# Modulation columns in whole tiles of 1024 instead of two halves of 512, with bias and scale for eight columns at once

## The chip, the cores and the metric

The kernel runs on one core of a Trainium2 chip. The core has five engines that run side by side, each with a queue of its own that it works off in order: TensorE (PE in the profile; its weight loads are PEld), VectorE (DVE), ScalarE (ACT), GpSimd (POOL) and SyncE (SP), which here issues nearly all DMA transfers. They wait for each other by semaphores. The metric is the time of one execution in device microseconds (us).

## The reference

A trunk of two layers over a sequence of 512 tokens with 1024 features, in float32. A vector `c` sets, per layer, six modulation vectors of 1024: shift, scale and gate for the attention, and the same for the MLP.

```python
sc = jax.nn.silu(c)
for layer in range(DEPTH):
    mod = sc @ w_mod[layer] + b_mod[layer]
    shift1, scale1, gate1, shift2, scale2, gate2 = [m[:, None, :] for m in jnp.split(mod, 6, axis=-1)]
    h = rmsnorm(x, g_attn[layer]) * (1.0 + scale1) + shift1
    o = mixer_layer(h, w_in[layer], w_out[layer], diff_lambda[layer], ...)
    x = x + gate1 * o
    h = rmsnorm(x, g_mlp[layer]) * (1.0 + scale2) + shift2
    up = h @ w_up[layer]
    u, g = up[..., :D_FF], up[..., D_FF:]
    g = causal_depthwise_conv(g, conv_w[layer], conv_b[layer])
    x = x + gate2 * ((jax.nn.silu(g) * u) @ w_down[layer])
return rmsnorm(x, g_final)
```

`mixer_layer` is one input projection, three kinds of attention heads (A differential, B dilated windows, C forgetting) and one output projection. The factor of the differential heads comes from `diff_lambda`.

## The kernel before

**Layout.** Features lie on the 128 partitions and tokens in the free dimension, so a vector of 1024 features is eight columns of a 128-row tile. Matrix products run at float32 accuracy as three products of split operands: each weight tile comes by DMA as `raww`, ACT rounds it to `whi` (line 174), DVE takes the rest as `wlo` (line 186), and `mm3` (lines 264 to 267) issues high x high, high x low and low x high. Activations are split in the same way (`hh` and `hl`, lines 313 and 314, for the normalised input).

**Stages.** Start-up computes shift1 and scale1 of layer 0 from the tiles `mu`. Then follow, for each layer, `layer_attn` and `layer_mlp`. In `layer_attn` a loop over `b` takes 64 blocks of attention (8 pairs of heads, 2 heads, 4 blocks of 128 queries) in a software pipeline: scores `s` (`emit_S`), their masked maximum on DVE (`emit_max`, line 653, `nm`), the exponential on ACT (`emit_exp`, line 666, `e`), for kind A a combination of two maps on DVE (`emit_norm`, lines 679 to 681, `rd`), the transposes on TensorE (`emit_T`, line 694, `pt`), their split into `pth` on ACT and `ptl` on DVE (lines 713 and 718), and the product with the values (`emit_PV`, lines 740 and 741, `po`). Between them `fill` puts the projections of the next heads. `head_post` finishes a head (`op`, line 753, and on).

**The modulation columns.** One column `ci` of the 48 of a layer is a dot product of 128 rows of `w_mod` (1024 long, `wmod[l, ci]`) with `silu(c)`, which `scb` holds on all partitions. `mod_col` (line 211) does it in two halves of 512. Each half is loaded into a tile `rawm` of the pool `mrp` (three buffers, line 240). In the attention of layer 0 (columns 16 to 39) POOL multiplies it with `scb` (line 221), ACT sums it by its accumulator (line 224), and DVE adds the sum to the bias or to the first half (line 226). Elsewhere, in the MLP of layer 0 (columns 40 to 47 and all 48 of layer 1), one DVE instruction does product and sum (line 228). The columns of the two scale vectors are turned into `scl = (1 + scale) * g` one by one (line 234). From then on `h_part` reads `modc` and `scl`, and `gated_add` (line 326) reads the gates.

**What sets the order.** `mod_gen` turns the columns into a generator of small steps. In the attention the loop over `b` takes `mr` = 3.2 steps per block from block `ms` = 4 on (lines 848 to 851); in the MLP each `tick()` takes one. A scheduler then puts each engine's instructions into its queue in an order of its own, by priority and by what it reckons to be ready; on the chip every queue is worked off strictly in that order. A load into a buffer that is still read waits in SP's queue, and so does all that stands behind it there.

`lp`, the tile for `diff_lambda`, is loaded at start-up (line 1061) and read by `prep` (line 366) in block 10 of layer 0.

## Time and profile before

| | us |
|---|---|
| median of 3 runs | 1345.78 (1345.72 to 1348.15) |
| span of the profiled execution, first to last instruction | 1343.3 |
| start-up, until the first score maximum | 70.2 |
| attention of layer 0, until its last `x` | 70.2 to 318.7 |
| MLP of layer 0 | to about 680 |
| attention of layer 1, until its last `x` | to 963.4 |
| MLP of layer 1 and final norm | to 1343.3 |

The profile gives no time of the profiled execution apart from its span; the median of the runs is 2.5 us above it. How to read the rows that follow: in the tables of groups a row has the line, the engine, the operation, output<-inputs, the shapes, the number of instructions, then their busy time and mean duration in ns, then the idle time of the engine ahead of them and what ended it. In the timelines a row has the start and the duration in us, and in brackets the idle time ahead. Durations of neighbours overlap a little; from start to start is how long an instruction holds its queue. Busy TensorE means that a matmul was in its pipeline.

The stretch of DVE's queue at which the attention of layer 0 ends and its MLP begins is one of the places that matter below; the first half columns of the MLP stand in it.

### The profile page before, as it was taken

How to read it: one execution, taken by the hardware profiler on the slowest of the kernel's cores; microseconds unless marked ns; L12 is line 12 of the kernel's file. 1: busy time of each engine (PE TensorE's matmuls, PEld its weight loads, DVE VectorE, ACT ScalarE, POOL GpSimd, SP SyncE). 2: the span in 40 equal slices, each digit the busy share in tenths (PEclk: the TensorE clock that was granted, in tenths of full speed). 3: DMA queues.
4: the chain of work that ended last, by engine and by line, in shares of the span. 5: the costliest groups of instructions: out<-in, count | busy, mean ns of one | idle time of the engine just before them, and what ended most of it. 6: DMA issues, size and time to landing. Idle time of an engine off the chain costs nothing.

```text
span 1343.3 us, 18226 instructions
## 1 busy us (share of the span) xinstructions
PE 1289.3 (96%) x6568; PEld 1058.5 (79%) x6568; DVE 869.7 (65%) x1733; ACT 663.8 (49%) x1242; POOL 92.3 (7%) x64
## 2 busy tenths in 40 slices
PE   3899898999999999999999999999999999999997
PEld 1678787688888888888898888878978888888886
DVE  7888989868888886422357687875754444443332
ACT  5567888954433333322345676775543333333231
POOL 5222423400000000000000000000000000000000
PEclk8899999999999999999999999999999999999999
DMA  9344453432777774233422234212123232222331
GB/s 374 142 142 150 162 155 130 133 116 85 252 250 257 249 252 139 91 98 99 130 83 94 85 105 123 79 59 83 54 94 94 95 96 97 100 91 91 101 100 63
DMA packets 68127, 174.44 MB, mean 130 GB/s; under 512 B 9410, under 2 KB 11730, under 8 KB 68036
## 3 DMA queue, kind: packets, MB, share of 16 engines
q1 hardware_dynamic: 66884, 172.16, 39.3%
q8 instruction: 52, 0.85, 0.3%
q10 hardware_dynamic: 1088, 1.05, 0.2%
q14 instruction: 39, 0.32, 0.1%
q0 software_dynamic: 64, 0.06, 0.0%
HBM read 159.41 MB, written 2.10 MB: 120 GB/s over the span
## 4 chain that ended last, share of the span: by engine, by line
PE 68%; DVE 5%; ACT 3%; issue 2%; DMA 1%; SPq 0%; DVEq 0%; ACTq 0%
PE pu L265 6%; PE pg L266 6%; PE pg L267 6%; PE pu L267 6%; PE pu L266 6%; PE pg L265 6%; PE dps L265 6%; PE dps L267 6%; PE dps L266 6%; PE qkps L265 2%; PE ops L266 2%; PE ops L265 2%; PE ops L267 2%; PE qkps L266 2%; PE qkps L267 2%
## 5 line engine op out<-in xcount | busy, mean ns | idle before, releaser
L186 DVE TENSOR_TENSOR wlo<-raww,whi 128x1024 fp32r<-128x1024 f32 (+3 forms) x188 | 229.5, 1221 | 238.2 <-ACT whi L174 234.2
L174 ACT ACTIVATE whi<-raww 128x1024 fp32r<-128x1024 f32 (+3 forms) x188 | 194.5, 1035 | 344.3 <-PE dps L266 138.0
L266 PE MATMUL pg<-hl,whi 128*128 128x512 f32 (+1 forms) x368 | 143.0, 389 | 0.4 <-DVE hl L314 0.2
L265 PE MATMUL pg<-hh,whi 128*128 128x512 f32 (+1 forms) x368 | 141.5, 385 | 1.6 <-ACT whi L174 1.6
L265 PE MATMUL pu<-hh,whi 128*128 128x512 f32 (+1 forms) x368 | 142.3, 387 | 0.0
L267 PE MATMUL pg<-hh,wlo 128*128 128x512 f32 (+1 forms) x368 | 140.9, 383 | 1.1 <-DVE wlo L186 1.1
L266 PE MATMUL pu<-hl,whi 128*128 128x512 f32 (+1 forms) x368 | 140.7, 382 | 0.0
L267 PE MATMUL pu<-hh,wlo 128*128 128x512 f32 (+1 forms) x368 | 140.6, 382 | 0.0
L265 PE MATMUL dps<-mh,whi 128*128 128x512 f32 x308 | 121.5, 395 | 0.0
L267 PE MATMUL dps<-mh,wlo 128*128 128x512 f32 x308 | 121.5, 394 | 0.0
L266 PE MATMUL dps<-ml,whi 128*128 128x512 f32 x308 | 121.2, 393 | 0.0
L666 ACT ACTIVATE e<-e,nm 128x256 f32<-128x256 f32 (+3 forms) x160 | 88.9, 556 | 32.4 <-DVE nm L653 30.5
L265 PE MATMUL qkps<-hh,whi 128*128 128x512 f32 x224 | 98.3, 439 | 0.6 <-ACT qf L467 0.2
L653 DVE CUSTOM_DVE_ANT_0 e<-s,cst 128x256 f32<-128x256 f32 (+3 forms) x160 | 76.8, 483 | 21.3 <-PE s L632 9.2
L906 ACT ACTIVATE y<-y 128x512 f32<-128x512 f32 x44 | 27.8, 632 | 126.3 <-DVE y L903 116.7
L266 PE MATMUL qkps<-hl,whi 128*128 128x512 f32 x224 | 89.5, 400 | 0.0
L267 PE MATMUL qkps<-hh,wlo 128*128 128x512 f32 x224 | 89.0, 397 | 0.0
L267 PEld LDWEIGHTS pu<-hh,wlo 128*128 128x128 f32 x368 | 69.1, 188 | 16.5 <-DVE wlo L186 1.1
L266 PEld LDWEIGHTS pg<-hl,whi 128*128 128x128 f32 x368 | 69.0, 188 | 16.6 <-DVE hl L314 2.0
L267 PEld LDWEIGHTS pg<-hh,wlo 128*128 128x128 f32 x368 | 69.0, 188 | 16.5 <-DVE wlo L186 1.9
L265 PEld LDWEIGHTS pg<-hh,whi 128*128 128x128 f32 x368 | 69.2, 188 | 16.0 <-ACT whi L174 2.0
L221 POOL TENSOR_TENSOR rawm<-rawm,scb 128x512 f32<-128x512 f32 x48 | 69.5, 1458 | 163.4 <-DMA rawm<-in_wmod_dram 119.5
(182 smaller groups left out, 2814.7 us busy)
## 6 DMA issues: line engine op xcount, KB each, us to landing
raww<-in_wup_dram SPq DMA_DIRECT2D x88, 512.0 KB
rawm<-in_wmod_dram SPq DMA_DIRECT2D x160, 256.0 KB
raww<-in_wqk_dram SPq DMA_DIRECT2D x32, 512.0 KB
raww<-in_wdown_dram SPq DMA_DIRECT2D x32, 512.0 KB
mu<-in_wmod_dram SPq DMA_DIRECT2D x16, 512.0 KB
raww<-in_wout_dram SPq DMA_DIRECT2D x16, 448.0 KB
raww<-in_wv_dram SPq DMA_DIRECT2D x12, 512.0 KB
raww<-in_wdown_dram SPq DMA_DIRECT2D x16, 384.0 KB
```

The costliest lines, as they stand in the source:

```text
L174: A.activation(out=h[:, 0:m], in_=self.raw[i][:, c:c + m], func=AF.Copy)
L186: V.tensor_tensor(out=lo[:, 0:m], in0=raw[:, c:c + m], in1=h[:, 0:m].bitcast(F32), op=ALU.subtract)
L221: G.tensor_tensor(out=raw, in0=raw, in1=scb[:, 512 * half:512 * half + 512], op=ALU.mult)
L265: T.matmul(ps[:, c], w[0], rhs[0][:, c], start=first, stop=False, skip_group_check=True)
L266: T.matmul(ps[:, c], w[0], rhs[1][:, c], start=False, stop=False, skip_group_check=True)
L267: T.matmul(ps[:, c], w[1], rhs[0][:, c], start=False, stop=last, skip_group_check=True)
L653: anchor[0] = V.tensor_tensor_reduce(out=e[:, 0:n], in0=s[:, 0:n], in1=cst[:, mask + SEQ - n:mask + SEQ], scale=-scale, scalar=3e38, op0=A ...
L666: anchor[1] = A.activation(out=e[:, 0:n], in_=e[:, 0:n], func=AF.Exp, bias=nm, scale=-1.0, accum_out=den).ins
L906: last_silu[0] = A.activation(out=y, in_=y, func=AF.Silu).ins
```

## The change

`mod_col` and `mod_stream` become one generator. A column is one tile of 128x1024, one load, and one instruction on POOL and on ACT, or one on DVE. The bias of columns 16 to 39, and the scales, are done for eight columns in one DVE instruction when the last of the eight is ready (`m` = 7). `mrp` has two buffers of 1024 instead of three of 512. `lp` is no longer a tile of its own: in block 6 it takes a buffer of `mrp`, is loaded there, and is read by `prep` in block 10. The columns are taken at `mr` = 1.3 steps per block, with three steps per column in place of eight.

```diff
@@ -63,7 +63,7 @@
     hs = ctx.enter_context(tc.tile_pool(name="hs", bufs=28))
     rawp = ctx.enter_context(tc.tile_pool(name="rawp", bufs=3))
     wp = ctx.enter_context(tc.tile_pool(name="wp", bufs=2))
-    mrp = ctx.enter_context(tc.tile_pool(name="mrp", bufs=3))
+    mrp = ctx.enter_context(tc.tile_pool(name="mrp", bufs=2))
     tp = ctx.enter_context(tc.tile_pool(name="tp", bufs=4))
     sp = ctx.enter_context(tc.tile_pool(name="sp", bufs=1))
     sm = ctx.enter_context(tc.tile_pool(name="sm", bufs=8))
@@ -107,7 +107,7 @@
     cb = const.tile([128, DEPTH, FC], F32, name="cb")
     sg = const.tile([128, DEPTH], F32, name="sg")
     fb = const.tile([128, DEPTH, 6], F32, name="fb")
-    lp = const.tile([128, DEPTH, 4, 32], F32, name="lp")
+    lpt = []
     modc = const.tile([128, DEPTH, 48], F32, name="modc")
     scl = const.tile([128, DEPTH, 2, KC], F32, name="scl")
     nlam = const.tile([128, DEPTH], F32, name="nlam")
@@ -208,38 +208,32 @@
 
     W = Weights()
 
-    def mod_col(l, ci, raws, pool=False):
+    def mod_stream(l, ci):
         part, m = divmod(ci, 8)
-        prev = bm[:, l, ci:ci + 1]
-        for half in range(2):
-            raw = raws(half)
-            yield
-            dst = modc[:, l, ci:ci + 1]
-            if half == 0:
-                dst = sm.tile([128, 1], F32, tag="mp", name="mp")
-            if pool:
-                G.tensor_tensor(out=raw, in0=raw, in1=scb[:, 512 * half:512 * half + 512], op=ALU.mult)
-                yield
-                d2 = sm.tile([128, 1], F32, tag="mp", name="mq")
-                A.activation(out=raw, in_=raw, func=AF.Copy, accum_out=d2)
-                yield
-                V.tensor_tensor(out=dst, in0=d2, in1=prev, op=ALU.add)
-            else:
-                V.tensor_tensor_reduce(out=raw, in0=raw, in1=scb[:, 512 * half:512 * half + 512], scale=1.0, scalar=prev,
-                                       op0=ALU.mult, op1=ALU.add, accum_out=dst)
-            prev = dst
-            yield
+        pool = l == 0 and 16 <= ci < 40
+        raw = mrp.tile([128, 1024], F32, tag="raw", name="rawm")
+        nc.sync.dma_start(out=raw, in_=wmod[l, ci])
+        yield
+        dst = modc[:, l, ci:ci + 1]
+        if pool:
+            G.tensor_tensor(out=raw, in0=raw, in1=scb, op=ALU.mult)
+            yield
+            A.activation(out=raw, in_=raw, func=AF.Copy, accum_out=dst)
+        else:
+            V.tensor_tensor_reduce(out=raw, in0=raw, in1=scb, scale=1.0, scalar=bm[:, l, ci:ci + 1],
+                                   op0=ALU.mult, op1=ALU.add, accum_out=dst)
+            yield
+            yield
+        yield
+        if m < 7:
+            return
+        c = slice(8 * part, 8 * part + 8)
+        if pool:
+            V.tensor_tensor(out=modc[:, l, c], in0=modc[:, l, c], in1=bm[:, l, c], op=ALU.add)
         if part in (1, 4):
             g = gA if part == 1 else gM
-            V.scalar_tensor_tensor(out=scl[:, l, part // 4, m:m + 1], in0=modc[:, l, ci:ci + 1], scalar=1.0,
-                                   in1=g[:, l, m:m + 1], op0=ALU.add, op1=ALU.mult)
-
-    def mod_stream(l, ci):
-        def raws(half):
-            raw = mrp.tile([128, 512], F32, tag="raw", name="rawm")
-            nc.sync.dma_start(out=raw, in_=wmod[l, ci, :, 512 * half:512 * half + 512])
-            return raw
-        return mod_col(l, ci, raws, l == 0 and 16 <= ci < 40)
+            V.scalar_tensor_tensor(out=scl[:, l, part // 4, :], in0=modc[:, l, c], scalar=1.0,
+                                   in1=g[:, l, :], op0=ALU.add, op1=ALU.mult)
 
     def mod_gen(units, off):
         for l, u in units:
@@ -364,6 +358,7 @@
         return st
 
     def prep():
+        lp = lpt[0]
         for l in range(DEPTH):
             lam_init = 0.8 - 0.6 * math.exp(-0.3 * l)
             V.tensor_scalar(out=sg[:, l:l + 1], in0=sg[:, l:l + 1], scalar1=1.0 - lam_init, scalar2=None, op0=ALU.mult)
@@ -820,6 +815,10 @@
             while idx and fills[idx - 1][0]:
                 fill(idx - 1, 1.0)
             p = b - lag
+            if l == 0 and b == 6:
+                lpt.append(mrp.tile([128, 1024], F32, tag="raw", name="lp")[:, 0:256].rearrange(
+                    "p (l j d) -> p l j d", l=DEPTH, j=4))
+                nc.sync.dma_start(out=lpt[0], in_=lamp)
             if l == 0 and b == 10:
                 with tc.issue_after(anchor[0]), tc.issue_after(anchor[1]):
                     prep()
@@ -845,7 +844,7 @@
             fill(idx, f3)
             if p >= 0:
                 emit_PV(p)
-            ms, mr = 4, 3.2
+            ms, mr = 4, 1.3
             if b >= ms:
                 for _ in range(int((b - ms + 1) * mr) - int((b - ms) * mr)):
                     next(modg, None)
@@ -1058,7 +1057,7 @@
             st = attn_init(0, unit, ps0)
             W.pt = None
             with tc.issue_after(last_load[0]):
-                for t, a in ((fb, fbias), (cst, consts), (lp, lamp), (sg, sublng), (gM, gmlp), (gF, gfin), (cw, convw),
+                for t, a in ((fb, fbias), (cst, consts), (sg, sublng), (gM, gmlp), (gF, gfin), (cw, convw),
                              (cb, convb)):
                     nc.sync.dma_start(out=t, in_=a)
         for l in range(DEPTH):
```

Where the order changes, at the places that the prediction uses. The rows are one engine's instructions in the order of its queue; a row has the line, the operation, output<-inputs and the shape (ISA is the DVE instruction of lines 228 and 653 and the read of its accumulator). Lines of the changed kernel stand some five lower between 240 and 815, so that its L308 is L314 before, and its L661 is L666.

DVE at the end of the norm that opens the MLP of layer 0, before:

```order
L314 SCALAR_TENSOR_TENSOR hl<-ht,modc,hh 128x256
L228 ISA rawm,modc<-rawm,scb,mp 128x512
L228 ISA modc 128x1
L314 SCALAR_TENSOR_TENSOR hl<-ht,modc,hh 128x256
L228 ISA rawm,mp<-rawm,scb,bm 128x512
L228 ISA mp 128x1
L228 ISA rawm,modc<-rawm,scb,mp 128x512
L228 ISA modc 128x1
L186 TENSOR_TENSOR wlo<-raww,whi 128x1024
```

The same place in the changed kernel:

```order
L308 SCALAR_TENSOR_TENSOR hl<-ht,modc,hh 128x256
L223 ISA rawm,modc<-rawm,scb,bm 128x1024
L223 ISA modc 128x1
L308 SCALAR_TENSOR_TENSOR hl<-ht,modc,hh 128x256
L223 ISA rawm,modc<-rawm,scb,bm 128x1024
L223 ISA modc 128x1
L186 TENSOR_TENSOR wlo<-raww,whi 128x1024
```

One whole column stands ahead of the last `hl` where a half stood, and one between it and `wlo` where two halves stood. A whole column also stands some sixteen rows earlier, behind the fourth `hl`, where the first half stood.

ACT in the first blocks of the attention of layer 0, from the first column on, before:

```order
L224 ACTIVATE rawm,mq<-rawm 128x512
L666 ACTIVATE e,dens<-e,nm 128x128
L174 ACTIVATE whi<-raww 128x1024
L666 ACTIVATE e,dens<-e,nm 128x256
L467 ACTIVATE qf<-qkps 128x512
L666 ACTIVATE e,dens<-e,nm 128x384
L666 ACTIVATE e,dens<-e,nm 128x512
L713 ACTIVATE pth<-pt 128x384
```

And in the changed kernel:

```order
L221 ACTIVATE rawm,modc<-rawm 128x1024
L661 ACTIVATE e,dens<-e,nm 128x128
L174 ACTIVATE whi<-raww 128x1024
L661 ACTIVATE e,dens<-e,nm 128x256
L462 ACTIVATE qf<-qkps 128x512
L661 ACTIVATE e,dens<-e,nm 128x384
L221 ACTIVATE rawm,modc<-rawm 128x1024
L708 ACTIVATE pth<-pt 128x384
```

The second column now stands ahead of `pth` and of the exponential of 128x512, which follows two rows later.

## The prediction

> **What bounds the kernel now.** I read the busy table first, then the busy time by stage, then TensorE's waits, and last the groups of instructions of the columns.

> ```profile
> PE 1289.3 (96%) x6568; PEld 1058.5 (79%) x6568; DVE 869.7 (65%) x1733; ACT 663.8 (49%) x1242; POOL 92.3 (7%) x64
> ...
> 75.00:325.00 250.00, 237.82 (x1416) 197.85 (x1414) 209.56 (x508) 189.38 (x450) 63.56 (x46) 1.00 0.42 135
> ...
> 345.00:680.00 335.00, 334.96 (x1474) 272.44 (x1473) 209.74 (x384) 109.14 (x137) 0.00 (x0) 1.00 0.55 177
> ...
> 705.00:955.00 250.00, 245.87 (x1441) 204.66 (x1441) 186.58 (x448) 164.97 (x361) 0.00 (x0) 0.99 0.28 89
> ```

> The columns of a stretch are its bounds, its length, the busy time of PE, PEld, DVE, ACT and POOL, then the granted clock, the share of the DMA engines and GB/s. TensorE is busy 96% of the span. From 345 to 680 us, the MLP of layer 0, it is busy 334.96 of 335.00 us: no engine or transfer that becomes cheaper there can shorten it. What can be won lies in the attention of layer 0 (75 to 325), with 12.18 us of idle TensorE, and the attention of layer 1 (705 to 955) is the yardstick: the same arithmetic, no modulation columns, 4.13 us idle. So the columns, with all that hangs on them, cost about 8.05 us of TensorE's time in layer 0. In those two stretches DVE is 22.98 us and ACT 24.41 us busier in layer 0.

> TensorE's waits from 75 to 325 us (total, times, longest):

> ```profile
> PE po L741 <- DVE ptl L718: 2.9, 3, 1.9
> PE pt L694 <- DVE e L681: 2.0, 1, 2.0
> PE po L740 <- DVE op L753: 1.9, 1, 1.9
> PE s L640 <- DVE nm L653: 1.4, 2, 0.8
> ```

> Three single waits of 2.0, 1.9 and 1.9 us make 5.8 of the 8.05 us, and all wait for DVE. They are traced below.

> **The change in the attention of layer 0.** These are the groups that go or change form (busy us, mean ns); the last four are the nearest rows for the new, wider forms.

> ```profile
> L226 DVE TENSOR_TENSOR modc<-mq,mp 128x1 f32<-128x1 f32 x24 | 9.0, 377 | 1.2 <-ACT rawm L224 1.1
> L226 DVE TENSOR_TENSOR mp<-mq,bm 128x1 f32<-128x1 f32 x24 | 7.7, 319 | 0.7 <-ACT rawm L224 0.6
> L234 DVE SCALAR_TENSOR_TENSOR scl<-modc,gM 128x1 f32<-128x1 f32 x8 | 3.4, 427 | 0.1
> L224 ACT ACTIVATE rawm<-rawm 128x512 f32<-128x512 f32 x48 | 29.8, 621 | 2.0 <-POOL rawm L221 1.9
> L224 ACT ACTIVATION_READ_ACCUMULATOR rawm<-rawm 128x1 f32 x48 | 9.1, 190 | 0.0
> L221 POOL TENSOR_TENSOR rawm<-rawm,scb 128x512 f32<-128x512 f32 x48 | 69.5, 1458 | 163.4 <-DMA rawm<-in_wmod_dram 119.5 <-ACT e L666 34.1 <-ACT whi L174 4.7
> ...
> L1044 POOL TENSOR_TENSOR mu<-mu,scb 128x1024 f32<-128x1024 f32 x8 | 20.9, 2646 | 14.5 <-DMA mu<-in_wmod_dram 14.5
> ...
> L1045 ACT ACTIVATE mu<-mu 128x1024 f32<-128x1024 f32 x8 | 8.4, 1044 | 3.1 <-POOL mu L1044 3.1
> ...
> L758 DVE RECIPROCAL dens<-dens 128x8 f32<-128x8 f32 x8 | 1.6, 195 | 0.0
> ```

> DVE loses 48 additions and 8 scales, 9.0 + 7.7 + 3.4 = 20.1 us, and gains three additions and one scale of eight columns; at the 195 ns of L758, the only form of 128x8, that is 0.8 us. Net -19.3. ACT goes from 29.8 + 9.1 = 38.9 us to 24 x (1.044 + 0.190) = 29.6 us, -9.3. POOL goes from 69.5 us to 24 x 2.646 = 63.5 us: the same work, in pieces 1.81 times as long. That length matters, because POOL holds DVE up:

> ```profile
> 210.57 2.52 POOL L221 TENSOR_TENSOR rawm<-rawm,scb 128x512 f32<-128x512 f32 x2 [3.53 <-ACT e L666]
> ...
> 210.62 1.26 DVE L680 SCALAR_TENSOR_TENSOR rd<-rd,nlam,dens 128x1 f32<-128x1 f32 x1
> 211.91 1.72 DVE L681 SCALAR_TENSOR_TENSOR e<-e,rd 128x512 f32<-128x512 f32 x1
> ...
> 213.78 0.63 PE L694 MATMUL pt<-cst,e 128*128 128x128 f32 x4 [1.96 <-DVE e L681]
> ...
> 149.27 2.12 DVE L186 TENSOR_TENSOR wlo<-raww,whi 128x1024 fp32r<-128x1024 f32 x1
> 151.31 1.22 DVE L680 SCALAR_TENSOR_TENSOR rd<-rd,nlam,dens 128x1 f32<-128x1 f32 x1
> ...
> 25.74 2.52 DVE L314 SCALAR_TENSOR_TENSOR hl<-ht,modc,hh 128x512 fp32r<-128x512 f32 x1
> ...
> L186 DVE TENSOR_TENSOR wlo<-raww,whi 128x1024 fp32r<-128x1024 f32 x20 | 29.6, 1478 | 3.1 <-ACT whi L174 3.0
> L680 DVE SCALAR_TENSOR_TENSOR rd<-rd,nlam,dens 128x1 f32<-128x1 f32 x16 | 5.7, 364 | 0.0
> ...
> L186 DVE TENSOR_TENSOR wlo<-raww,whi 128x1024 fp32r<-128x1024 f32 x21 | 25.6, 1220 | 10.9 <-ACT whi L174 10.9
> L680 DVE SCALAR_TENSOR_TENSOR rd<-rd,nlam,dens 128x1 f32<-128x1 f32 x16 | 3.4, 215 | 0.1
> ```

> The first four rows are one event. A 128x1 operation takes 1.26 us because it started just behind a POOL multiplication and could not end before it; the next one is caught by the second multiplication, and TensorE waits 1.96 us. The wait of 1.9 us for `op` follows the rows at 149.27 and 151.31, of the same kind. At start-up, where POOL already works on 1024 columns, `hl` took 2.52 us in the same way (row 25.74). The four groups, layer 0 above and layer 1 (no POOL work) below, give the sum over two operations: `wlo` 20 x (1.478 - 1.220) = 5.2 us and `rd` 16 x (0.364 - 0.215) = 2.4 us, together 7.6 us of DVE held up in operations that stay. With the new pieces the chance of meeting one goes with POOL's busy time (63.5 / 69.5 = 0.91) and the wait with the length of a piece (1.81), a factor of 1.66: +5.0 us. The bounds are a factor of 0.91 (-0.7 us), if only busy time counts, and 1.81 (+6.2 us), if as many operations are caught as now.

> [...]

> So DVE is relieved by 19.3 - 5.0 = 14.3 of its 22.98 us (62%), ACT by 9.3 of 24.41 (38%). What reaches TensorE has two ends. If its idle time follows the mean relief of 50%, 4.0 of the 8.05 us go. If the three waits behind held-up operations grow by 0.66 x 5.8 = 3.8 us, and the relief acts on the other 2.25 us alone (-1.1), the stage becomes 2.7 us longer. I take the middle, **-0.6 us**: most of the hold-ups already vanish in TensorE's backlog, but the expensive ones are of this kind.

> **The change at the start of the MLP of layer 0.** There DVE sets the pace, and the columns stand in its queue among the `hl` that TensorE waits for.

> ```profile
> 318.26 0.48 DVE L326 SCALAR_TENSOR_TENSOR x<-ops,modc,x 128x256 f32<-128x256 f32 x1
> ...
> 329.71 0.75 DVE L228 CUSTOM_DVE_ANT_0 rawm<-rawm,scb,mp 128x512 f32<-128x512 f32 x1
> ...
> 330.38 0.48 DVE L314 SCALAR_TENSOR_TENSOR hl<-ht,modc,hh 128x256 fp32r<-128x256 f32 x1
> ...
> 332.43 1.22 DVE L186 TENSOR_TENSOR wlo<-raww,whi 128x1024 fp32r<-128x1024 f32 x1
> ...
> 962.94 0.48 DVE L326 SCALAR_TENSOR_TENSOR x<-ops,modc,x 128x256 f32<-128x256 f32 x1
> ...
> 976.29 1.23 DVE L186 TENSOR_TENSOR wlo<-raww,whi 128x1024 fp32r<-128x1024 f32 x1 [1.60 <-ACT whi L174]
> ...
> L228 DVE CUSTOM_DVE_ANT_0 rawm<-rawm,scb,mp 128x512 f32<-128x512 f32 x54 | 40.5, 750 | 13.3 <-DMA rawm<-in_wmod_dram 12.5
> ...
> L256 DVE TENSOR_TENSOR ml<-y,mh 128x512 fp32r<-128x512 f32 x17 | 11.7, 686 | 0.0
> ```

> From the last `x` to the first `wlo` behind it it takes 14.17 us in layer 0 and 13.35 us in layer 1, where no columns stand: two half columns before the last `hl` cost 0.82 us. A half holds the queue for 330.38 - 329.71 = 0.67 us. A whole one is not in the trace: it lies between 0.67 (width free) and 1.34 us (two halves). The step from 512 to 1024 in a plain DVE operation is 1220 - 686 = 534 ns, so I take 0.67 + 0.53 = 1.20 us. The order now puts two whole columns where two halves stood, so 2 x 0.53 = **+1.06 us** on the chain that ends in `wlo` (bounds 0 and +1.34); the slack that the halves used is gone. The third column, behind the last `hl`, has the place of two halves and stays beside ACT's `whi`, for which `wlo` waits anyway.

> **At nothing:** the rest of the MLP. DVE sheds 56 x (2 x 0.75 - 1.28) = some 12 us there, under a TensorE that is never idle, and the transfers keep their bytes, under a DMA share of 0.55; were that cover gone, a late weight would show as a wait of `pg` or `pu` for `whi`. The load of `lp` leaves start-up, where TensorE waits for other things.

> **Sum:** -0.6 + 1.06 = +0.5 us on a span of 1343.3 us. The runs' median, 1345.78 us, lies 2.5 us above that span, and I keep this difference: **1346.3 us**. About 0.2%, 2.7 us, is what a measurement can tell from no change.

> **The rivals.** *Faster:* relief reaches TensorE, and two thirds of the excess go: -5.4 + 1.06 = -4.3, 1341.5 us. For it speaks that DVE runs at 84% in this stage; against it, that ACT is relieved by a third only. *Slower:* POOL's longer hold-ups of `wlo`, `rd` and `e` in the stages of kind A pass TensorE's backlog, from about 1.5 us on: +2.7 + 1.06 = +3.8, 1349.6 us. At its upper factor, 0.81 x 5.8 - 1.1 + 1.06 = +4.7, 1350.4 us. *The streams stand:* while `lp` holds one of the two buffers, the second column's load waits for ACT's pass over the first, and ACT, in order, waits for the second column ahead of `pth` and an `e`.

> ```profile
> 67.80 1.22 SPq L240 DMA_DIRECT2D rawm<-in_wmod_dram  x2
> ...
> 71.88 3.51 POOL L221 TENSOR_TENSOR rawm<-rawm,scb 128x512 f32<-128x512 f32 x2 [5.57 <-DMA rawm<-in_wmod_dram]
> ...
> 75.41 0.72 ACT L666 ACTIVATE e<-e,nm 128x512 f32<-128x512 f32 x1 [1.86 <-DVE nm L653]
> ```

> From the issue to the end of both halves on POOL it takes 75.39 - 67.80 = 7.6 us; issued 1 to 2 us later, the column ends at about 77, so ACT stands some 2 us past 75.41. Added to the forecast, 0 to 2 us: 1346.3 to 1348.3 us, still within 0.2%.

> **Chances:** the forecast 0.37, the streams 0.08, faster 0.27, slower 0.28. So faster by over 0.2% 0.27, within 0.2% 0.45, slower 0.28. The range takes 80% of the excess as gain at one end (-6.4 + 1.06, 1340.5 us) and the slower rival at its upper factor with 1.6 us of standing streams at the other: 1340.5 to 1352.0 us; within the forecast alone 1343.1 to 1348.5 us.

> **What would show it.** Right: TensorE idle near 11 to 13 us from 75 to 325 us; `rd` and `wlo` there with means above 364 and 1478 ns; no L226; the stretch from `x` to `wlo` near 15.2 us; TensorE still busy from 345 to 680. Wrong: idle below 8 us (faster), above 15 us (slower), waits of ACT for `rawm` well over 2 us (streams), or a wait in the MLP for a weight.

## The result and the profile after

| | us |
|---|---|
| before, median of 4 runs | 1346.97 (1345.72 to 1350.61) |
| after, median of 4 runs | 1368.97 (1367.08 to 1370.49) |
| ratio after / before | 1.0143, 95% interval 1.0112 to 1.0173 |
| predicted | 1346.3, range 1340.5 to 1352.0 |
| span of the profiled execution after (its own time) | 1364.9 (1367.08) |

The change makes the kernel 1.4% slower, and the time lies 17 us above the range. First the same views as in the prediction: the busy line of the page, and the stretches by stage (bounds, length, busy PE, PEld, DVE, ACT, POOL, granted clock, DMA share, GB/s) of the changed kernel.

```profile
PE 1301.7 (95%) x6568; PEld 1066.0 (78%) x6568; DVE 861.7 (63%) x1555; ACT 659.1 (48%) x1194; POOL 88.8 (7%) x40
...
75.00:325.00 250.00, 233.26 (x1322) 192.46 (x1321) 200.98 (x428) 177.22 (x384) 63.17 (x24) 0.97 0.43 134
345.00:680.00 335.00, 330.39 (x1420) 264.94 (x1419) 204.71 (x273) 110.20 (x137) 0.00 (x0) 1.00 0.56 176
```

DVE, ACT and POOL are all less busy over the span, as the change promised. Yet TensorE is idle for 16.7 us of the first stretch (12.18 before) and for 4.6 of the second (0.04 before), where part of it is the transition's end, which comes later now. The first also has a granted clock of 0.97. TensorE is *more* busy over the whole span than before (1301.7 against 1289.3 us) with the same 6568 matmuls: some ran at half clock (the mean granted clock of the span is 0.983, before 0.991).

To split the 21.6 us between the two spans I cut both profiles at the same events: the first score maximum, the first `pg`, the first long run of `pu`, and the first `x` of the MLP's down projection (582.16 us before, so the row of the MLP ends there and not at its last `x`). Idle time is the length less TensorE's busy time; the loss to the clock is an estimate, half of TensorE's busy time within the stretches that the trace records at a granted clock of 0.5: after, two 128x512 matmuls in a row start 427 ns apart in them and 231 ns elsewhere (medians).

| stretch | before | after | more | idle, before to after | half clock, before to after |
|---|---|---|---|---|---|
| start-up, to the first maximum | 70.20 | 71.39 | +1.2 | | |
| attention of layer 0 | 246.80 | 259.52 | **+12.7** | 12.1 to 17.2 | 0 to 6.5 |
| transition | 21.89 | 22.95 | **+1.06** | 1.6 to 2.7 | 0 to 0 |
| MLP of layer 0 | 243.27 | 247.87 | **+4.6** | 0.04 to 2.7 | 0 to 0 |
| the rest | 761.19 | 763.22 | +2.0 | 16.0 to 15.2 | 1.7 to 5.1 |

Between the marks of the attention DVE is no less busy than before, 206.96 us against 205.38 (the row of before stands further down, above that of eight_act):

```profile
71.39:330.91 259.52, 242.33 (x1379) 200.48 (x1380) 206.96 (x443) 183.71 (x399) 63.69 (x24) 0.97 0.42 131
```

**In the attention** these are TensorE's waits from 60 to 380 us (total, times, longest), one of ACT's, and groups from 75 to 325 us.

```profile
PE s L635 <- DVE nm L648: 3.3, 4, 2.2
PE po L736 <- DVE ptl L713: 3.1, 5, 0.9
PE pt L689 <- DVE ptl L713: 3.1, 1, 3.1
PE pt L689 <- DVE e L676: 3.1, 2, 1.9
...
ACT rawm L221 <- POOL rawm L219: 13.1, 12, 2.2
...
L186 DVE TENSOR_TENSOR wlo<-raww,whi 128x1024 fp32r<-128x1024 f32 x18 | 27.9, 1550 | 3.5 <-ACT whi L174 3.5
...
L676 DVE SCALAR_TENSOR_TENSOR e<-e,rd 128x512 f32<-128x512 f32 x4 | 7.2, 1794 | 0.1
L675 DVE SCALAR_TENSOR_TENSOR rd<-rd,nlam,dens 128x1 f32<-128x1 f32 x16 | 6.9, 432 | 0.1
...
L219 POOL TENSOR_TENSOR rawm<-rawm,scb 128x1024 f32<-128x1024 f32 x23 | 63.5, 2772 | 112.7 <-DMA rawm<-in_wmod_dram 96.2 <-ACT e L661 6.1 <-ACT pth L708 5.3
```

`rd` and `wlo` are longer than before (364 and, in the same stretch, 1381 ns), the 512 wide `e` too (986 ns). POOL's pieces take 2772 ns (I had 2646), and ACT now stands 13.1 us for POOL, 12 times (1.9 us, 4 times before). The longest wait, 3.1 us, shows how POOL makes it; rows are start, duration, instruction, and in brackets the idle time ahead:

```profile
175.86 5.16 POOL L219 TENSOR_TENSOR rawm<-rawm,scb 128x1024 f32<-128x1024 f32 x2 [3.53 <-DMA rawm<-in_wmod_dram]
...
175.95 2.85 DVE L250 TENSOR_TENSOR qf<-qf,sw 128x512 fp32r<-128x512 f32 x1
178.72 3.38 DVE L186 TENSOR_TENSOR wlo<-raww,whi 128x1024 fp32r<-128x1024 f32 x1
182.02 0.54 DVE L713 TENSOR_TENSOR ptl<-pt,pth 128x384 fp32r<-128x384 f32 x1
...
182.62 1.11 PE L689 MATMUL pt<-cst,e 128*128 128x128 f32 x4 [3.12 <-DVE ptl L713]
...
181.05 1.06 ACT L221 ACTIVATE rawm<-rawm 128x1024 f32<-128x1024 f32 x1 [1.33 <-POOL rawm L219]
```

Two whole columns stand back to back on POOL (one row, x2). Each catches one DVE instruction: `qf` takes 2.85 us (0.68 without POOL), `wlo` 3.38 (1.22 without). `ptl`, behind both, is late, and TensorE with it. ACT meanwhile waits for the second column. And what follows is new:

```profile
175.32:178.74 3.42, 3.42 (x26) 2.94 (x25) 3.42 (x5) 3.42 (x8) 2.88 (x2) 1.00 0.53 184
178.74:182.15 3.41, 0.76 (x7) 0.56 (x5) 3.41 (x3) 2.08 (x5) 2.28 (x1) 1.00 0.45 130
182.15:185.56 3.41, 2.94 (x14) 2.94 (x15) 3.41 (x8) 2.92 (x7) 0.00 (x0) 0.50 0.40 99
185.56:188.98 3.42, 3.42 (x29) 3.38 (x29) 2.54 (x6) 2.22 (x6) 0.00 (x0) 1.00 0.08 19
```

The stretches of 3.41 us around that wait: TensorE is busy for 0.76 us in one, and is granted half clock (0.50) in the next. After has four such stretches at half clock in this stage, at 93, 148, 182 and 216 us, before has none. In the 3.41 us ahead of the last three TensorE was busy for 1.44, 0.76 and 1.60 us; these three cost 4.8 of the 6.5 us. Ahead of the one at 93 us it was busy all the time, so no wait explains that one (the last section comes back to it).

**In the MLP** it is another chain: two waits from 345 us on, then one place.

```profile
PE pu L261 <- DVE wlo L186: 2.5, 7, 0.5
...
DVE rawm L223 <- DMA rawm<-in_wmod_dram: 22.2, 31, 2.1
...
427.77 1.29 DVE L223 CUSTOM_DVE_ANT_0 rawm<-rawm,scb,bm 128x1024 f32<-128x1024 f32 x1 [0.36 <-DMA rawm<-in_wmod_dram]
...
430.30 1.28 DVE L223 CUSTOM_DVE_ANT_0 rawm<-rawm,scb,bm 128x1024 f32<-128x1024 f32 x1 [0.57 <-DMA rawm<-in_wmod_dram]
...
432.11 1.22 DVE L186 TENSOR_TENSOR wlo<-raww,whi 128x1024 fp32r<-128x1024 f32 x1
...
433.38 0.50 PE L261 MATMUL pu<-hh,wlo 128*128 128x512 f32 x1 [0.44 <-DVE wlo L186]
```

DVE, in order, waits for the loads of whole columns ahead of `wlo`, and `wlo` comes 0.44 us too late. TensorE meets this seven times. (The 4.6 us of the stage are more than these 2.5. The ends of matmuls are modelled in the profile, so part of a wait may be shown as busy; that is not settled.) Waiting for loads is not new in itself: before, DVE stood 18.2 us for 25 loads in the same stretch, and TensorE waited for no `wlo` there. What is new is where these waits fall.

### The profile page after: what moved, and what is told of

The parts are those of the page before. It is cut to its first block, busy times and chain, and to the rows that moved or that the text cites. A ratio compares the mean times of both kernels' runs of the same rounds, so it can differ in the third digit from the quotient of the medians.

```text
span 1364.9 us, 17762 instructions
## 1 busy us (share of the span) xinstructions
PE 1301.7 (95%) x6568; PEld 1066.0 (78%) x6568; DVE 861.7 (63%) x1555; ACT 659.1 (48%) x1194; POOL 88.8 (7%) x40
## 4 chain that ended last, share of the span: by engine, by line
PE 56%; DMA 7%; DVE 6%; ACT 3%; issue 2%; DVEq 0%; SPq 0%; ACTq 0%
DMA rawm<-in_wmod_dram 6%; PE dps L259 6%; PE dps L261 6%; PE dps L260 6%; PE pu L259 4%; PE pu L261 4%; PE pu L260 4%; PE pg L260 4%; PE pg L261 4%; PE pg L259 4%; PE qkps L259 2%; PE qkps L260 2%; PE qkps L261 2%; DVE rawm L223 1%; DVE wlo L186 1%
## 5 line engine op out<-in xcount | busy, mean ns | idle before, releaser
L186 DVE TENSOR_TENSOR wlo<-raww,whi 128x1024 fp32r<-128x1024 f32 (+3 forms) x188 | 232.2, 1235 | 247.3 <-ACT whi L174 241.8
L174 ACT ACTIVATE whi<-raww 128x1024 fp32r<-128x1024 f32 (+3 forms) x188 | 194.4, 1034 | 331.8 <-PE dps L260 137.8
L661 ACT ACTIVATE e<-e,nm 128x256 f32<-128x256 f32 (+3 forms) x160 | 88.9, 556 | 44.0 <-DVE nm L648 42.3
L223 DVE CUSTOM_DVE_ANT_0 rawm<-rawm,scb,bm 128x1024 f32<-128x1024 f32 x56 | 71.7, 1281 | 22.7 <-DMA rawm<-in_wmod_dram 22.2
```

Source lines behind the costliest of these rows:

```text
L174: A.activation(out=h[:, 0:m], in_=self.raw[i][:, c:c + m], func=AF.Copy)
L186: V.tensor_tensor(out=lo[:, 0:m], in0=raw[:, c:c + m], in1=h[:, 0:m].bitcast(F32), op=ALU.subtract)
L223: V.tensor_tensor_reduce(out=raw, in0=raw, in1=scb, scale=1.0, scalar=bm[:, l, ci:ci + 1], op0=ALU.mult, op1=ALU.add, accum_out=dst)
L661: anchor[1] = A.activation(out=e[:, 0:n], in_=e[:, 0:n], func=AF.Exp, bias=nm, scale=-1.0, accum_out=den).ins
```

## The experiments

All times are medians, and ratios are to the kernel before, run on the same chip in the same job. The median of before moves from job to job (1346.97 to 1349.59 us), so rows are compared by their ratios. Theories A to D are named in the expectations. The table has each profile's attention of layer 0 (length, TensorE idle, lost to half clock), ACT's waits for POOL there, and DVE's hold-ups: by how much instructions that overlap a column on POOL ran longer than the same form elsewhere.

| kernel | us | ratio (95%) | attention | idle | half clock | ACT waits | DVE held | MLP |
|---|---|---|---|---|---|---|---|---|
| before | | 1 | 246.8 | 12.1 | 0 | 1.9 | 24.9 | 243.3 |
| after | 1368.97 | 1.0143 (1.0112 to 1.0173) | 259.5 | 17.2 | 6.5 | 13.1 | 30.5 | 247.9 |
| pool_halves | 1368.32 | 1.0143 (1.0119 to 1.0166) | 262.4 | 18.4 | 6.8 | 16.8 | 27.3 | 248.0 |
| act_late | 1367.88 | 1.0146 (1.0123 to 1.0168) | 257.2 | 17.4 | 5.1 | 2.5 | 25.4 | 247.6 |
| mlp_pace | 1365.55 | 1.0124 (1.0104 to 1.0145) | 263.2 | 16.5 | 10.9 | 13.0 | 34.7 | 242.6 |
| combo | 1354.62 | 1.0040 (1.0026 to 1.0054) | 251.0 | 12.4 | 1.7 | 1.8 | 18.0 | 242.6 |
| combo_mr12 | 1351.30 | 1.0025 (1.0002 to 1.0047) | 251.1 | 11.2 | 5.1 | 0 | 18.7 | 242.6 |
| after_mr12 | 1374.85 | 1.0190 (1.0167 to 1.0213) | 265.6 | 17.0 | 14.6 | 15.4 | 27.4 | 246.7 |
| before_mr30 | 1343.15 | 0.9971 (0.9952 to 0.9989) | 244.6 | 9.5 | 0 | 1.7 | 20.2 | 243.1 |
| eight_only | 1361.48 | 1.0086 (1.0057 to 1.0115) | 261.9 | 15.8 | 11.4 | 11.5 | 20.6 | 244.6 |
| eight_act | 1348.35 | 0.9995 (0.9977 to 1.0013) | 246.3 | 9.4 | 3.4 | 0 | 16.7 | 246.6 |
| dve_cols | 1349.20 | 0.9999 (0.9981 to 1.0018) | 243.5 | 6.1 | 3.4 | none | none | 250.7 |
| dve_pace | 1340.94 | 0.9952 (0.9932 to 0.9972) | 241.9 | 6.1 | 1.7 | none | none | 242.6 |
| dve_late | 1340.37 | 0.9938 (0.9916 to 0.9960) | 241.8 | 6.1 | 1.7 | none | none | 242.6 |

The losses to half clock differ from one execution to the next: mlp_pace has the attention of the changed kernel, instruction for instruction, and its profile lost 10.9 us where that of after lost 6.5, so the stage took 263.2 us against 259.5. The idle time (16.5 against 17.2) is the steadier column.

**POOL's pieces alone.**

```diff
-            G.tensor_tensor(out=raw, in0=raw, in1=scb, op=ALU.mult)
+            for q in (slice(0, 512), slice(512, 1024)): G.tensor_tensor(out=raw[:, q], in0=raw[:, q], in1=scb[:, q], op=ALU.mult)
```

> The changed kernel, with POOL's multiplication of a column as two instructions of 512 columns on the same tile; loads, buffers, ACT and the columns of the MLP stay. Theory A (the longer POOL pieces hold DVE up, and TensorE behind it): the hold-ups of wlo, rd and e fall back towards 13 us, at least two of the long waits of TensorE near 146, 161 and 180 us go, and the end of layer 0's attention comes 6 to 12 us earlier: 1357 to 1363 us. Theory B (ACT stands for POOL's whole column ahead of pth and e): POOL needs 2 x 1.46 = 2.9 us instead of 2.7 for a column, ACT still waits for both halves, so the time stays at 1367 to 1372 us.

The time is the one that theory B gave. Of theory A the single waits come true, but not the sum: DVE's hold-ups go from 30.5 to 27.3 us, far from 13, and the same attention in another execution (mlp_pace) has 34.7. At the place shown above, the same `qf` and `wlo` in pool_halves, then two of ACT's passes, and a `ptl` behind the first of them:

```profile
177.28 1.12 DVE L250 TENSOR_TENSOR qf<-qf,sw 128x512 fp32r<-128x512 f32 x1
179.68 2.20 DVE L186 TENSOR_TENSOR wlo<-raww,whi 128x1024 fp32r<-128x1024 f32 x1 [1.27 <-ACT whi L174]
...
173.71 1.06 ACT L221 ACTIVATE rawm<-rawm 128x1024 f32<-128x1024 f32 x1 [1.79 <-POOL rawm L219]
...
183.04 1.06 ACT L221 ACTIVATE rawm<-rawm 128x1024 f32<-128x1024 f32 x1 [1.99 <-POOL rawm L219]
...
175.40 0.56 DVE L713 TENSOR_TENSOR ptl<-pt,pth 128x384 fp32r<-128x384 f32 x1 [1.18 <-ACT pth L708]
```

`qf` falls from 2.85 to 1.12 us and `wlo` from 3.38 to 2.20; the waits near 146, 161 and 180 us fall from 2.17, 1.85 and 3.12 to 1.22, 0.91 and 1.57. But ACT stands longer for the two halves, and `ptl` waits for ACT's `pth`. What the shorter pieces give, ACT's standing takes.

**ACT's pass alone.** The pass comes a step later and is tied behind the newest exponential in ACT's queue. (The column's last step goes for it, so a column still takes three.)

```diff
             G.tensor_tensor(out=raw, in0=raw, in1=scb, op=ALU.mult)
-            yield
-            A.activation(out=raw, in_=raw, func=AF.Copy, accum_out=dst)
+            yield; yield
+            with tc.issue_after(anchor[1]): A.activation(out=raw, in_=raw, func=AF.Copy, accum_out=dst)
```

> The changed kernel, with ACT's pass over a column one step later and held behind the newest exponential in ACT's queue; POOL's pieces stay 1024 columns long. Theory B (ACT stands for POOL): ACT's waits for POOL at L221 fall from 13.1 us (12) to under 3 us, and the end of layer 0's attention comes 4 to 10 us earlier: 1359 to 1365 us. Theory A (POOL's pieces hold DVE up): the waits for POOL go, but the hold-ups of wlo, rd and e stay near 30 us and the time at 1366 to 1371 us.

ACT's waits fall to 2.5 us as meant, and the time stays: the outcome of theory A, though DVE's hold-ups (25.4 us) are below the 30 it named. POOL's whole columns still do this, here on POOL, DVE and TensorE of act_late:

```profile
233.41 2.42 POOL L219 TENSOR_TENSOR rawm<-rawm,scb 128x1024 f32<-128x1024 f32 x1 [4.91 <-DMA rawm<-in_wmod_dram]
...
233.62 2.75 DVE L428 TENSOR_TENSOR qk<-qf,qk 64x512 fp32r<-64x512 f32 x1
...
237.02 0.66 PE L689 MATMUL pt<-cst,e 128*128 128x128 f32 x4 [2.03 <-DVE ptl L713]
```

So undoing either one alone gives no time back: with what is left of the other, TensorE still has waits of 1.6 to 2 us.

**The pace of the MLP's columns.**

```diff
-            yield
-            yield
+            yield; yield
+            yield; yield
```

> The changed kernel, with six steps for a column in the MLP of layer 0 instead of four, so that the 56 columns take some 255 us instead of 170; the attention stays. Theory C (DVE stands in its queue for the load of a whole column, ahead of wlo, and TensorE waits for wlo): the seven waits of pu for wlo between 405 and 495 us go, the stretch from 352 us to the end of the MLP is 4 to 5 us shorter, 1364 to 1366 us. Rival (the wide operations are in the way by their length, 1.28 us, not by their loads): the same 56 operations still stand ahead of wlo, some waits remain, and the time is 1368 to 1370 us.

Theory C holds. The stretch of mlp_pace from 345 to 680 us, with TensorE's and DVE's waits from 345 or 352 to 600:

```profile
345.00:680.00 335.00, 333.04 (x1453) 270.49 (x1452) 209.79 (x283) 114.69 (x142) 0.00 (x0) 1.00 0.55 177
...
PE pg L261 <- DVE wlo L186: 0.5, 1, 0.5
...
DVE rawm L223 <- DMA rawm<-in_wmod_dram: 10.3, 13, 0.9
```

DVE's standing for loads halves, `pu` waits for `wlo` no more (the wait left is `pg`'s, in the transition), and the stage takes 242.6 us, below before's 243.3. The same 56 wide operations are in it, so their length is not what hurt. The median fell by 3.4 us, as expected, though the intervals of the two ratios overlap; the stage is the firmer evidence.

**Both in the attention, and the pace.** The three edits above in one kernel.

> The changed kernel with three edits at once: POOL's multiplication in two instructions of 512 columns, ACT's pass held behind the newest exponential and a step later, six steps for a column in the MLP. If POOL's piece length, ACT's standing and the pace of the MLP are the causes, each with its own share, TensorE's idle time from the first score maximum to the MLP falls from 17.2 to 12 or 13 us, fewer windows of half clock follow, and the time is 1346 to 1354 us. If they stand in for each other, or if the order of the attention's instructions as such is the cause, the MLP's share alone comes back: 1362 to 1367 us.

Idle 12.4 us, and 1354.62 us, just above the expected 1346 to 1354: in the attention both causes have to go. Against mlp_pace, which has the same pace in the MLP, the two edits bring the ratio from 1.0124 to 1.0040, some 11 us. combo and after differ in order as well as in these causes, so the next three ask what order alone does.

```diff
-            ms, mr = 4, 3.2
+            ms, mr = 4, 3.0
```

> The kernel before with one number changed: 3.0 steps of the columns in a block instead of 3.2. Every instruction, tile and load is the same; only the places of the columns' steps and with them the order in the queues move. Theory D (the time of this stage is set by where the order puts the waits, and a wait of about 2 us costs as much again in half clock): the idle time from the first maximum to the MLP changes by 2 us or more, one to four windows of half clock appear, and the time is 1352 to 1362 us. Rival (the changed kernel loses by its longer pieces, fewer buffers or missing additions, not by order): 1345 to 1350 us.

```diff
-            ms, mr = 4, 1.3
+            ms, mr = 4, 1.2
```

> The changed kernel with 1.2 steps of the columns in a block instead of 1.3, so that the last pooled column ends in the same block as in the kernel before (72 steps in 60 blocks, as 192 at 3.2). Theory D (order decides): the waits fall elsewhere, and the time moves by 3 us or more, to either side. Rival (piece length and buffers decide, whatever the order): within 3 us of the changed kernel, 1366 to 1372 us.

> The kernel combo (POOL in two pieces, ACT's pass held, slower MLP columns) with 1.2 steps in a block instead of 1.3, as after_mr12 stands to the changed kernel. If the three edits remove causes, the gain holds at this other order too: some 14 to 20 us below after_mr12 (1374.9), 1353 to 1361 us. If combo only met a good order, it falls back to 1362 us or more.

Order alone moved the idle time of the kernel before by 2.7 us, as theory D has it, but downwards: no half clock in this stage, and 0.3% *faster* (1343.15 against 1348.06 us in the same job), which neither expectation had. That the kernel before merely stood at a good order gets no support from this one other order. The changed kernel at the other pace became slower (ratio 1.0190 after 1.0143; the intervals overlap a little), as D has it, but with the same idle time (17.0 us) and more half clock. At this pace too the three edits bring the ratio down, from 1.0190 to 1.0025; the median, 1351.30 us, is below the expected 1353 to 1361. At both paces tried the change loses and the edits win most of it back; a size of some 5 us hangs on the order and the clock.

**The additions alone.** Before's tiles, pieces and loads; the halves' sums are kept apart and added for eight columns, and the scale is set for eight.

```diff
...
-                V.tensor_tensor(out=dst, in0=d2, in1=prev, op=ALU.add)
...
+        if m < 7:
+            return
+        c = slice(8 * part, 8 * part + 8)
+        if pool:
+            V.tensor_tensor(out=modc[:, l, c], in0=modc[:, l, c], in1=mhalf, op=ALU.add)
+            V.tensor_tensor(out=modc[:, l, c], in0=modc[:, l, c], in1=bm[:, l, c], op=ALU.add)
...
```

> The kernel before, with three buffers of 512 columns and its pieces, but the sums of the pooled columns added for eight columns at once (two additions of 128x8 instead of 48 of 128x1 for 24 columns) and the scale of eight columns at once. DVE is relieved by some 18 us in the attention of layer 0, POOL, ACT and the loads as before. If DVE's relief reaches TensorE (the part of my forecast that counted it), the 12.2 us of idle TensorE there fall to 8 or 9: 1342 to 1344 us. If the waits are set by what stands ahead in the queues, and not by DVE's total, it stays at 1346 to 1348 us.

Both expectations missed: 11.9 us slower than before, with short pieces and three buffers. One event of eight_only, and the wait of TensorE that it ends in:

```profile
242.59 0.63 ACT L222 ACTIVATE rawm<-rawm 128x512 f32<-128x512 f32 x1 [2.91 <-POOL rawm L220]
...
243.87 1.01 DVE L261 TENSOR_TENSOR ol<-op,oh 128x512 fp32r<-128x512 f32 x1 [3.18 <-ACT oh L259]
...
PE s L635 <- DVE nm L658: 3.8, 1, 3.8
```

Without the additions the scheduler puts ACT's passes where ACT has to wait for POOL (11.5 us), `oh` stands behind the pass, `ol` behind `oh`, and the next maximum behind `ol`. If that is all, tying the pass behind the newest exponential must cure it:

```diff
-                A.activation(out=raw, in_=raw, func=AF.Copy, accum_out=mhalf[:, m:m + 1] if half else dst)
+                with tc.issue_after(anchor[1]): A.activation(out=raw, in_=raw, func=AF.Copy, accum_out=mhalf[:, m:m + 1] if half else dst)
```

> The kernel eight_only (tiles of 512 and three buffers as before, sums and scale for eight columns at once; 1361.5 us) with ACT's passes held behind the newest exponential in its queue. If eight_only lost by ACT standing for POOL (11.5 us in 9 waits there, against 1.9 us in 4 in the kernel before), the waits fall under 3 us, and with DVE's relief left the time is 1342 to 1349 us. If the missing additions shifted the order on DVE alone, it stays at 1355 to 1364 us.

It does: ACT's waits for POOL are gone, and the ratio falls from 1.0086 to 0.9995. It also prices DVE's relief. The attention of before and of eight_act, in the columns of the stages:

```profile
70.20:317.00 246.80, 234.66 (x1380) 194.16 (x1380) 205.38 (x495) 187.65 (x447) 66.69 (x47) 1.00 0.43 136
...
70.12:316.42 246.30, 236.95 (x1383) 197.10 (x1382) 195.24 (x446) 187.10 (x449) 65.52 (x47) 0.99 0.43 136
```

DVE is 10.1 us less busy, TensorE's idle time falls from 12.1 to 9.4 us, and the time of the kernel doesn't change (0.9995): half clock in this stage (3.4 us) and 3.3 us more in the MLP took it. The 2.7 us by which order alone moved the idle time are as much, so even this gain is not surely the relief's. The loss in the MLP is of the kind seen in after (three waits of `pu` for `wlo`, 2.4 us), with halves of 512 and three buffers. Ahead of each of the three `wlo` DVE had stood 0.9 to 2.6 us for a load. So it takes no whole columns; it takes a load that DVE stands for at the wrong place.

**No POOL and no ACT in the columns.** DVE reduces the pooled columns in one instruction each. A column now takes four steps instead of three, so 1.6 steps are taken per block.

```diff
-        pool = l == 0 and 16 <= ci < 40
+        pool = False
...
-            ms, mr = 4, 1.3
+            ms, mr = 4, 1.6
```

> The changed kernel with the 24 pooled columns reduced by DVE in one instruction each, as in the MLP (POOL and ACT have no part in them; four steps for a column, 1.6 steps in a block). DVE takes over 24 x 1.28 = 30.7 us and loses the hold-ups by POOL (about 30 us in the changed kernel), ACT loses 29.6 us. If POOL's lock and ACT's standing make the loss of the attention, TensorE's idle time there falls to 10 to 13 us and the time is 1351 to 1359 us (the MLP's loss stays). If order decides, the idle time stays at 15 to 19 us: 1362 to 1372 us.

POOL's lock in it means the hold-ups of DVE in the table (30.5 us after). The idle time falls to 6.1 us, half of before's and below the expected 10 to 13, with DVE's busy time as before (204.8 us): the columns cost DVE what POOL's hold-ups and the additions had. The two buffers of 1024 and the place of `lp` are still those of the changed kernel, so by themselves they cost the attention nothing that shows here. This kernel, too, stands at an order of its own, but neither change of pace above moved the idle time by more than 2.7 us. The MLP's loss is still in it (7.4 us here), and the next two take it and the transition's away. dve_pace has the six steps in the MLP; dve_late also starts the MLP's columns later:

```diff
     def mod_gen(units, off, start=0):
+        for _ in range(start): yield
...
-                    aux.append(mod_gen([(0, u) for u in range(40, 48)] + [(1, u) for u in range(48)], 200))
+                    aux.append(mod_gen([(0, u) for u in range(40, 48)] + [(1, u) for u in range(48)], 200, 16))
```

> The kernel dve_cols (the pooled columns reduced by DVE, 1.6 steps in a block) with six steps for a column in the MLP of layer 0. The two causes lie in different stages, so their gains should add: dve_cols took 253.5 us from the start of the MLP's long part to its end, mlp_pace 245.4. Expected: 245 to 246 us there, and 1342 to 1346 us. If the columns' loads only move their collisions to later weights, the time stays at 1347 to 1350 us.

> The kernel dve_pace with the stream of the MLP's columns begun 16 steps later, so that no column stands among the hl of the transition (in the changed kernel two whole columns stand there). The transition's terms of the prediction, 0.82 us for two halves in the kernel before and 1.06 us for their doubled width, should both go: the stretch from the last x to the first wlo becomes about 13.4 us plus at most one column (1.2 us), TensorE's idle time in the transition falls from 2.67 us to 0.8 to 1.6, and the time is 1 to 2 us below dve_pace. If those idle times have another cause, no difference from dve_pace within 0.5 us in the profile.

The gains add: 1340.94 us for dve_pace, below the expected 1342 to 1346. In dve_late no column stands among the `hl`; from the last `x` over one column to the first `wlo`:

```profile
312.24 0.48 DVE L321 SCALAR_TENSOR_TENSOR x<-ops,modc,x 128x256 f32<-128x256 f32 x1
...
323.91 1.27 DVE L223 CUSTOM_DVE_ANT_0 rawm<-rawm,scb,bm 128x1024 f32<-128x1024 f32 x1
...
325.60 1.22 DVE L186 TENSOR_TENSOR wlo<-raww,whi 128x1024 fp32r<-128x1024 f32 x1 [0.41 <-ACT whi L174]
```

That is 13.36 us, and the transition takes 21.06 us instead of 22.95. Idle time there is 1.56 us. Between the medians of dve_late and dve_pace lie 0.6 us, less than the two intervals can tell apart; the stage shows the gain, the runs don't. Both kernels beat before and after.

## Why the prediction was wrong, step by step

- **The step that failed is "The change in the attention of layer 0", -0.6 us; measured +12.7.** It was the middle of two ends, relief (-4.0) and longer hold-ups (+2.7). The measured value lies far outside both. Idle time makes some 5 us of it and half clock 6.5.
  - *Hold-ups.* The factor for `rd` and `wlo` was about right: 7.6 us grew to 11.4 (16 `rd`, 20 `wlo`), a factor of 1.5 where I had 1.66. But I counted two operations. In all operations that stay the hold-ups were 13.3 us before, and after they are 30.5 us (some 2 of them in the new additions of eight columns), up to 2.2 us in one. Two whole columns back to back, which catch two instructions ahead of one `ptl`, were not thought of.
  - *ACT.* I counted its lighter load and nothing for its order. It stood 13.1 us for POOL. Where I looked for this, at `lp` in block 6, it came as worked out (2.2 us, up to 76.9 us), but as a rival of 0.08 and at that place only; eleven more came later. With one of the two causes undone (act_late, pool_halves) the loss stays; with both undone (combo) 8.5 of the 12.7 us come back.
  - *Clock.* That a stretch with long waits is followed by half clock was in none of the cases: 4.8 us here. (The other 1.7 of the 6.5 us follow a stretch without waits.) The profile of before had waits of 1.9 to 2.0 us with none behind them, and I took their price to be their length.
- **The relief of DVE did not come.** I had 14.3 us net. In the attention after the change DVE is busy for 206.96 us, against 205.38 before: the longer hold-ups used the relief up. The term was also too large: I added up durations of neighbours that overlap (20.1 us), and in the profile of before only 13.4 us of DVE's busy time hang on these 56 operations. And where relief did come, in eight_act, 10.1 us less DVE gave 2.8 us less idle time and no measurable time.
- **The transition was right:** +1.06 us predicted, 22.95 - 21.89 = +1.06 measured, and the stretch from the last `x` to `wlo` took 15.23 us (15.2 forecast). dve_late took away 1.89 where two halves (0.82) and their doubling (1.06) make 1.88. The wide operation takes 1281 ns; I had 1.28 us.
- **"At nothing: the rest of the MLP" failed, +4.6 us.** I argued from a TensorE never idle and a DMA share of 0.55. The share stayed (0.56), yet DVE's queue stood for each load in turn, and `wlo` was behind it. The sign that I named for a lost cover was a wait for `whi`; the wait that came was for `wlo`, the low part of the same weight, and I gave it no chance.
- **The slower rival** had the right place (`wlo`, `rd`, `e` behind POOL) and the right sign, at 0.28, but its price, +3.8 to +4.7 us, took neither ACT nor the clock. That TensorE's backlog covers some 1.5 us was an estimate that no run shows; what showed is a wait of 3.1 us behind two hold-ups of 2.2 us (`qf` 2.85 against 0.68, `wlo` 3.38 against 1.22).
- *Not settled:* the 4.2 us of the attention that combo does not win back; where the 1.2 us of start-up come from; how much of the difference between after_mr12 and combo_mr12 (ratios 1.0190 and 1.0025) is the edits and how much the phase of the clock.

## What to carry to other kernels

Merging two instructions on a helper engine lengthened the time for which one of them blocks the others (here 1458 to 2772 ns); look at what stands behind it in each in-order queue, its consumer's too, before counting the instructions saved. A queue that is no bound by its busy share still set the time here where one of its instructions waited for a load or for another engine ahead of work that the bound engine needed. When several single causes are undone one at a time without effect, undo them together before dropping them.

## What the runs showed of the hardware

The 19 windows above 75% have something else in common: each holds 8 to 20 of the 40 matmuls `pf`, which are only six columns wide (128x6) and come in two groups, near 90 and near 735 to 765 us. Of the 17 windows that hold 14 or more of them, 16 were followed by half clock, though the profile shows TensorE busy in them. The stretch at 93 us after is one of these. Before, the same group at 88 to 91 us lay astride two windows and no half clock followed, so these 1.7 us are a matter of phase and not of the change.

All this was read from the profiles, and no experiment forced it. The longest single wait ahead of the stretch at 148 us was 2.17 us, less than one window.

The hold-ups between POOL and DVE show from POOL's side as well: its multiplication of 1024 takes 2372 ns at best and 3412 at worst, and the five longest (3.2 us and more) all began while a `wlo` of DVE was still running.
